# Hybrid encoder block: keys of memory heads 2 and 3 moved behind the query tiles, a12 loaded in another buffer, the last adds of the down-projection spread

## The chip, the cores and the metric

One core of a Trainium2 chip runs the whole kernel in one launch. The metric is device time in microseconds, lower is better; the kernel before takes 2694.26 us (median of three runs, 2693.18 to 2695.48).

## The reference, cut to what matters

The block works on 2048 tokens of width 1024, with a memory of 256 rows, in fp32:

```python
h  = rms_norm(x, mix_norm);  z = h @ w_in           # conv gates, q, k, v, g, low-rank gates
x += concat(convs, gated linear attention) @ w_out
hq = rms_norm(x, xa_norm) @ w_xq
km, vm = split(rms_norm(mem, mem_norm) @ w_xkv)     # 4 heads of 256
x += softmax(hq km' / 16) vm @ w_xo                 # memory cross-attention
x += square(relu(rms_norm(x, mlp_norm) @ w_up)) @ w_down
return rms_norm(x, final_norm)
```

## The kernel before, in words

Every fp32 operand of a product is split into a high part (a cast on ACT, L117) and a rest (a subtraction on DVE, L118); a product is then three matmuls per 128 rows (L145 to L147, `mm3`), so PE does three passes and is fed by one ACT and one DVE instruction per operand tile. Tokens come in four blocks of 512, in two halves (`hf`). A block is loaded in four tiles (`prep_load`), squared on ACT (L184) and folded on DVE (L188, L189), its norm is spread to all partitions by PE (`rstd_col` L161, `to_rows` L169, with a power on POOL, L153, in between), and `block_steps` scales it (eight L206 on DVE) and splits it (four casts on ACT, four L118 on DVE).

The prologue makes `zA`, the memory keys folded into the query weight. `kv_mm` (48 matmuls) makes a head's keys K0 to K3, `kv_out` (L552 and a split) scales them, `xa_key` multiplies them with two weights of `wxqT` in eight steps of six matmuls, and L565 evacuates each step. All four heads are made before `qk(0)`, which computes four query and key tiles for token blocks 0 and 1. Then come `lr_g` and `vg` (gates and values), `conv`, the V phase (`kv_mm` of `wxv` and `xa_value` for four heads, beside the preparation of blocks 2 and 3), `qk(1)`, the gated linear attention, and the cross-attention.

The MLP uses Strassen-like forms with seven products. `token_side` (up-projection) makes the token operands of a half; `quarter` loads a quarter of `x2d` and scales it; a12 is the last of the four quarters and takes its buffer `S2` (ring ST) after a11 has been used. In the down-projection `half_steps` yields 56 steps of up to 48 matmuls (L1243); `add` (L928) evacuates them into `acc`, sixteen tiles loaded from `x2d` by `load_acc`. POOL and DVE combine raw operands there. What is common to several quarters is collected in `sums` and added to `acc` by 24 adds on DVE after the steps. The last four feature rows of the hidden layer (REST) go through `column`: eight tiles of 12 matmuls for each of the token blocks, then `finish` scales and stores.

The order of work: PE's order is written out in the prologue, in the V phase and in the final columns (`manual_schedule`); the other engines, and PE elsewhere, are ordered by the scheduler, which fixes each engine's queue before the run. Every engine, and SP that issues the loads and stores, takes its queue in order: an instruction that waits holds all behind it.

Of the kernel before, what the change touches and what calls it, by code (L numbers as in the profile page):

```python
# [30 lines left out]
def block_kernel(ctx, tc, x, mem, wm, wv, wlg, wlog, wout, wxk, wxv, wxqT, wxo, wup, wdn,  # L31
# [195 lines left out]
    def qk(hf, blks, ws):  # L227
        t0 = hf * 1024
        for pr in range(2):
            for z, idx, sc in ((zk, 2 + pr, 1.0), (zq, pr, 0.125)):  # L230
                def ev(bi, ps, z=z, sc=sc):
                    t = T2()
                    nc.scalar.mul(t, ps, sc)
                    nc.sync.dma_start(z[pr][:, t0 + bi * TB:t0 + (bi + 1) * TB], t)
                mtiles([(idx, ev)], blks, ws)
                ws = None

# [511 lines left out]

    def block_sq(b, eng):  # L750
        xs = prep_load(x, b, lambda i: A2())
        return xs, fold(xs, A2, eng)

# [11 lines left out]
    with tc.manual_schedule(engines={EngineType.PE}):  # L765
        mts = [mem_part(0)]
        ws = [load_w(wxk[0])]
        mts.append(mem_part(1))
        ws.append(load_w(wxk[1]))
        nc.sync.dma_start(cst, consts)  # L770
        mps = kv_mm(wxk, 0, G4, ws)
        sq = fold([mt[:, 2 * j:2 * j + 2] for mt in mts for j in range(2)], lambda: T2(F32, (P, 2, NMEM)), nc.vector)
        nc.scalar.copy(rmem, to_rows(rstd_col(sq, PS), PS))
        K0 = kv_out(mps)
        K1 = kv_mm(wxk, 1, A4)
        xa_key(0, K0, G4)
# [4 lines left out]
        ws = [load_w(wxk[6 + j], T=A4) for j in range(2)]  # L781
        rc0 = rstd_col(sq0, PG)
        xa_key(1, K1, G4)
        with behind("dma", "act"):
            xs1, sq1 = block_sq(1, nc.vector)
        r0 = block_rows(rc0, PG)
        K2 = kv_out(K2)
        K3 = kv_mm(wxk, 3, A4, ws)
        xa_key(2, K2, G4)
        blks = [block_steps(xs0, r0)]  # L790
        rc1 = rstd_col(sq1, PG)
        K3 = kv_out(K3)
        r1 = block_rows(rc1, PG)
        xa_key(3, K3, G4)
        w0 = [load_w(wm[2])]
        blks.append(block_steps(xs1, r1))
    qk(0, blks, w0)
    vg(0, blks, lr_g(0, blks))
    conv(0, blks, range(4))
    with tc.manual_schedule(engines={EngineType.PE}):  # L800
        V0 = kv_mm(wxv, 0, G4)
        V1 = kv_mm(wxv, 1, G4)
        V0 = kv_out(V0)
        xa_value(0, V0, G4)
        with behind("dma", "act"):
            xs0, sq0 = block_sq(2, nc.vector)
        V1 = kv_out(V1)
        V2 = kv_mm(wxv, 2, G4)
        rc0 = rstd_col(sq0, PG)
        xa_value(1, V1, G4)  # L810
        with behind("dma", "act"):
            xs1, sq1 = block_sq(3, nc.vector)
        r0 = block_rows(rc0, PG)
        V2 = kv_out(V2)
        V3 = kv_mm(wxv, 3, G4)
        xa_value(2, V2, G4)
# [397 lines left out]
    def load_acc(ds):  # L1214
        for d in ds:
            for c in range(2):
                acc[d][c] = A4()
                nc.sync.dma_start(acc[d][c], x2d[d * P:(d + 1) * P, c * 1024:(c + 1) * 1024])

    halves = [slice(0, TB), slice(TB, 2 * TB)]  # L1220
    steps = half_steps()
    ahead = [next(steps)]
    acc = [[None, None] for _ in range(KT)]
    load_acc(range(4))
    sums = [A4(F32, (P, 2, TB)) for _ in range(4)]
    for i in range(14 * len(GROUPS)):
        while len(ahead) < 3:
            ahead.append(next(steps, None))
        first, p, c, w, x = ahead.pop(0)
        if i == 0:  # L1230
            load_acc(range(4, KT))
        n = len(x)
# [4 lines left out]
        for d in range(4):  # L1237
            ds = slice(d * P, (d + 1) * P)
            ps = banks[d]
            for k in range(n):  # L1240
                wh, wl = w[k][0][:, ds], w[k][1][:, ds]
                for l, r in ((wh, x[k][0]), (wh, x[k][1]), (wl, x[k][0])):
                    nc.tensor.matmul(ps, l, r, start=not chained and k == 0 and l is wh and r is x[k][0],  # L1243
                                     stop=k == n - 1 and l is wl, skip_group_check=chained)
            o11, o21 = (acc[d][c][:, h] for h in halves)
            o12, o22 = (acc[d + 4][c][:, h] for h in halves)
# [4 lines left out]
            for o in {1: (u,), 2: (o11,), 6: (u,), 5: (o22,), 3: (o12,), 7: (o21, o22), 4: (o21,)}[p]:  # L1251
# [6 lines left out]
    def rest_u(b):  # L1258
        got = []
        for i in range(0, 4, 2):  # L1260
            t = (RAW() if i == 0 else CV()[:, :D]).rearrange("p (j t) -> p j t", j=2)
            for j in range(2):
                f = REST[i + j]
                nc.sync.dma_start(t[:, j], zu[f * P:(f + 1) * P, b * TB:(b + 1) * TB])
            hi, lo = (A4(F32R, (P, 2, TB)) for _ in range(2))
            split(t, hi, lo)
            got += [(hi[:, j], lo[:, j]) for j in range(2)]
        return got

    ur = [rest_u(0)]  # L1270
    wr = [load_w(wdn[f], T=G4) for f in REST]
# [17 lines left out]

    def column(us, c, cs, squares, between):  # L1290

        qs = []
        n = cs.stop - cs.start
        o = cs.start % TB
        for d in range(KT):
            ds = slice(d * P, (d + 1) * P)
            ps = (PG if d % 2 == 0 else PS)()[:, :n]
            for j in range(4):
                mm3(ps, (wr[j][0][:, ds], wr[j][1][:, ds]), (us[j][0][:, o:o + n], us[j][1][:, o:o + n]), j == 0, j == 3)
# [24 lines left out]
    with tc.manual_schedule(engines={EngineType.PE, EngineType.DVE}):  # L1324
        for n, (c, cs) in enumerate(blocks):
            if n + 1 < 4:
                ur.append(rest_u(n + 1))
            sq = column(ur[min(n, 3)], c, cs, nc.vector if n == len(blocks) - 1 else nc.gpsimd, todo)
            for _ in todo or ():
# [64 lines left out]
```

## Time and profile before

| | us |
|---|---|
| median of three runs | 2694.26 |
| profiled execution | 2702.45 |
| its span | 2700.7 |
| PE busy | 2592.5 (96%) |
| DVE busy | 1626.4 (60%) |
| ACT busy | 933.2 (35%) |
| POOL busy | 259.6 (10%) |

The profiled execution is 1.75 us longer than its span, and 8.2 us above the median of the runs. PE is the engine that is busy nearly all of the span, so the table is read by what is left of it: 108.2 us in which PE is idle, a good part of it in a few places that the rows below show, and the stretches in which PE runs at the lower of its two clock levels.

### The profile page before, as it was taken

Reading aid. Unit: us, or ns where it says so; the run is one execution under the profiler, and the core shown is the slowest. Engines: PE = TensorE matmul, PEld = TensorE weight load, DVE = VectorE, ACT = ScalarE, POOL = GpSimd, SP = SyncE. Lnnn points to the kernel's source line nnn. Section 1 sums busy time; section 2 is a strip of 40 time slices with the busy share of each in tenths; the row PEclk is TensorE's granted clock in tenths of the full one; section 3 lists DMA queues with packets and bytes.
Section 4 is the critical chain, followed back from the end, with each engine's and each line's share of the span. In section 5 each row is a group of like instructions: output and inputs, shape, how many; then the busy total and the mean of one; then the engine's idle time right before and its main releaser. Section 6 shows DMA issues by size and latency. Waiting matters only on the chain.

```text
span 2700.7 us, 34654 instructions
## 1 busy us (share of the span) xinstructions
PE 2592.5 (96%) x13560; PEld 2207.7 (82%) x13560; DVE 1626.4 (60%) x2502; ACT 933.2 (35%) x1432; POOL 259.6 (10%) x178
## 2 busy tenths in 40 slices
PE   7999999989989999999999999899999899999998
PEld 7898888877777787989997888788887788888877
DVE  6512363467766455344467657766556768687975
ACT  5411153434435343232234333433333223222232
POOL 0000000000010000000000000000003224243223
PEclk9999999999999999999999999999999999999999
DMA  7512354224435452111134333343338664555233
GB/s 253 179 61 69 101 185 162 81 88 121 135 104 175 145 183 94 52 43 48 48 115 166 106 113 106 110 159 107 112 121 290 220 197 150 179 168 174 95 106 110
DMA packets 198309, 353.26 MB, mean 131 GB/s; under 512 B 17345, under 2 KB 73793, under 8 KB 198145
## 3 DMA queue, kind: packets, MB, share of 16 engines
q1 hardware_dynamic: 198144, 351.05, 39.9%
q8 instruction: 106, 1.74, 0.3%
q14 instruction: 59, 0.48, 0.1%
HBM read 262.90 MB, written 88.08 MB: 130 GB/s over the span
## 4 chain that ended last, share of the span: by engine, by line
PE 77%; DVE 10%; DMA 6%; ACT 3%; issue 2%; POOL 0%; SPq 0%; DVEq 0%; POOLq 0%; ACTq 0%
PE ps L1013 12%; PE ps L145 9%; PE ps L147 9%; PE ps L146 9%; PE pg L1243 9%; PE ps L1243 9%; PE pg L1013 9%; PE pg L145 3%; PE pg L147 3%; PE pg L146 2%; DVE a L118 2%; DMA gt<-zv 2%; DVE g L118 1%; DVE st L474 1%; DVE g L400 1%
## 5 line engine op out<-in xcount | busy, mean ns | idle before, releaser
L145 PE MATMUL ps<-a,a 128*128 128x512 f32 (+1 forms) x840 | 306.0, 364 | 6.5 <-DVE t L249 5.9
L146 PE MATMUL ps<-a,a 128*128 128x512 f32 (+1 forms) x840 | 306.0, 364 | 0.0
L147 PE MATMUL ps<-a,a 128*128 128x512 f32 (+1 forms) x840 | 305.1, 363 | 0.0
L1243 PE MATMUL pg<-a,g 128*128 128x512 f32 x1176 | 288.6, 392 | 10.1 <-DVE a L928 7.2
L1013 PE MATMUL ps<-a,g 128*128 128x512 f32 x1152 | 284.5, 392 | 7.4 <-ACT a L117 4.4
L1243 PE MATMUL ps<-a,g 128*128 128x512 f32 x1176 | 284.8, 389 | 0.0
L1013 PE MATMUL pg<-a,g 128*128 128x512 f32 x1152 | 279.6, 390 | 1.7 <-ACT g L117 1.1
L1243 PEld LDWEIGHTS pg<-a,g 128*128 128x128 f32 x1176 | 221.7, 189 | 59.1 <-issue 7.6
L1013 PEld LDWEIGHTS ps<-a,g 128*128 128x128 f32 x1152 | 217.4, 189 | 54.1 <-ACT a L117 5.0
L1243 PEld LDWEIGHTS ps<-a,g 128*128 128x128 f32 x1176 | 220.8, 188 | 45.9
L1013 PEld LDWEIGHTS pg<-a,g 128*128 128x128 f32 x1152 | 216.4, 188 | 48.4 <-ACT g L117 2.0
L117 ACT CAST a<-raw 128x1024 fp32r<-128x1024 f32 (+1 forms) x126 | 127.9, 1022 | 346.0 <-PE ps L1243 112.1
L118 DVE TENSOR_TENSOR a<-raw,a 128x1024 fp32r<-128x1024 f32 (+1 forms) x126 | 156.0, 1246 | 117.3 <-ACT a L117 115.9
L117 ACT CAST g<-gt 128x512 fp32r<-128x512 f32 x180 | 103.8, 618 | 349.0 <-PE pg L1013 197.2
L145 PEld LDWEIGHTS ps<-a,a 128*128 128x128 f32 x840 | 161.6, 192 | 32.6 <-DVE t L249 4.7
L146 PEld LDWEIGHTS ps<-a,a 128*128 128x128 f32 x840 | 162.0, 193 | 23.2 <-issue 0.2
L147 PEld LDWEIGHTS ps<-a,a 128*128 128x128 f32 x840 | 161.7, 192 | 23.3 <-issue 0.2
L118 DVE TENSOR_TENSOR g<-gt,g 128x512 fp32r<-128x512 f32 x180 | 133.4, 780 | 44.7 <-ACT g L117 44.7
L928 POOL TENSOR_TENSOR gt<-gt,t 128x512 f32<-128x512 f32 x42 | 79.4, 1908 | 815.9 <-DMA t<-in_wdn 746.9
L928 DVE TENSOR_TENSOR t<-pg,t 128x512 f32<-128x512 f32 x64 | 44.2, 691 | 172.0 <-issue 126.3
L928 DVE TENSOR_TENSOR a<-pg,a 128x512 f32<-128x512 f32 (+1 forms) x128 | 84.1, 668 | 62.3 <-PE pg L1243 46.1
L118 DVE TENSOR_TENSOR g<-raw,g 128x1024 fp32r<-128x1024 f32 (+3 forms) x90 | 98.7, 1107 | 35.6 <-ACT g L117 35.5
(323 smaller groups left out, 5157.7 us busy)
## 6 DMA issues: line engine op xcount, KB each, us to landing
raw<-zu SPq DMA_DIRECT2D x64, 512.0 KB, 4.1
t<-in_wdn SPq DMA_DIRECT2D x84, 256.0 KB, 4.1
raw<-in_wm SPq DMA_DIRECT2D x32, 512.0 KB, 4.1
raw<-in_wup SPq DMA_DIRECT2D x32, 512.0 KB, 4.1
cv<-in_wup SPq DMA_DIRECT2D x32, 512.0 KB, 4.9
zu<-gt SPq DMA_DIRECT2D x64, 256.0 KB, 2.4
zu<-t SPq DMA_DIRECT2D x64, 256.0 KB, 3.9
cv<-zu SPq DMA_DIRECT2D x32, 512.0 KB, 5.0
```

The source lines that it names most:

```text
L117: mark["act"] = nc.scalar.copy(hi, src)
L118: nc.vector.tensor_tensor(out=lo, in0=src, in1=hi.bitcast(F32), op=ALU.subtract)
L145: nc.tensor.matmul(ps, lh, rh, start=first, stop=False)
L146: nc.tensor.matmul(ps, lh, rl, start=False, stop=False)
L147: mark["pe"] = nc.tensor.matmul(ps, ll, rh, start=False, stop=last)
L400: nc.vector.tensor_tensor_scan(out=Q[hf][:, sl], data0=reset, data1=K[hf][:, sl], initial=0.0, op0=ALU.mult, op1=ALU.add)
L474: nc.vector.scalar_tensor_tensor(out=St[r, a], in0=St[r, b], scalar=de[r, a:a + 1], in1=St[r, a], op0=ALU.mult, op1=ALU.add)
L928: eng.tensor_tensor(out=out, in0=a, in1=b, op=op)
L1013: nc.tensor.matmul(ps, W[w][:, ks], X[x][kt], start=first and kt + w + x == 0, stop=kt == 3 and w == 1, skip_group_check=not first)
L1243: nc.tensor.matmul(ps, l, r, start=not chained and k == 0 and l is wh and r is x[k][0], stop=k == n - 1 and l is wl, skip_group_check=chained)
```

## The change

Five edits. (1) In the prologue blocks 0 and 1 are loaded and folded earlier, only heads 0 and 1 have their keys made before `qk(0)`; heads 2 and 3 follow it. (2) `qk` takes all four weights at once and runs four tiles on block 0, then four on block 1, where before each tile ran on both blocks. (3) Block 2 is loaded, folded and normed around the last convolution group of the first half, and the V phase prepares only block 3. (4) In the second half's up-projection a12 is loaded with the other quarters into `R2` (rings RAW and CV). (5) In the down-projection the first and second half of `acc` are loaded at steps 0 and 2 (before: ahead of the loop and at step 0), the first REST operands are loaded two steps before the end, the 24 adds move into `column`, one a tile, and the first column is made in two passes over all eight PSUM banks.

```diff
@@ qk
-        for pr in range(2):
-            for z, idx, sc in ((zk, 2 + pr, 1.0), (zq, pr, 0.125)):
-                mtiles([(idx, ev)], blks, ws)
+        tiles = [(i, out(z, i % 2, sc)) for i, z, sc in ((2, zk, 1.0), (0, zq, 0.125), (3, zk, 1.0), (1, zq, 0.125))]
+        mtiles(tiles, blks, ws + [load_w(wm[i]) for i, _ in tiles[1:]])
@@ prologue
         K0 = kv_out(mps)
+        with behind("dma", "act"):
+            xs0, sq0 = block_sq(0, nc.vector)
         K1 = kv_mm(wxk, 1, A4)
         xa_key(0, K0, G4)
-        with behind("dma", "act"):
-            xs0, sq0 = block_sq(0, nc.vector)
-        K1 = kv_out(K1)
-        K2 = kv_mm(wxk, 2, A4)
...
+        K1 = kv_out(K1)
         r0 = block_rows(rc0, PG)
...
         blks = [block_steps(xs0, r0)]
+        xa_key(1, K1, G4)
+        w0 = [load_w(wm[2])]
         rc1 = rstd_col(sq1, PG)
...
     qk(0, blks, w0)
+    for h in (2, 3):
+        xa_key(h, kv_out(kv_mm(wxk, h, A4)), G4)
     vg(0, blks, lr_g(0, blks))
-    conv(0, blks, range(4))
+    conv(0, blks, range(3))
+    xs0, sq0 = block_sq(2, nc.vector, lambda dt=F32: G4(dt, (P, 2, TB)))
+    r0 = block_rows(rstd_col(sq0, PG), PG)
+    conv(0, blks, [3])
+    blks = [block_steps(xs0, r0)]
@@ token_side
+        if hf == 1:
+            a12 = quarter(hf, 0, 1, R2())
         yield None
...
-        a12 = quarter(hf, 0, 1, S2())
+        if hf == 0:
+            a12 = quarter(hf, 0, 1, S2())
@@ down-projection
-    load_acc(range(4))
...
-        if i == 0:
-            load_acc(range(4, KT))
+        if i in (0, 2):
+            load_acc(range(2 * i, 2 * i + 4))
+        if i == 14 * len(GROUPS) - 2:
+            ur = [rest_u(0)]
+            wr = [load_w(wdn[REST[0]], T=G4)]
...
-    for d in range(4):
-        for c in range(2):
-            u = sums[d][:, c]
-            for o in (acc[d][c][:, halves[1]], acc[d + 4][c][:, halves[0]], acc[d + 4][c][:, halves[1]]):
-                add(o, o, u, eng=nc.vector)
@@ column
+        for d in range(KT if passes == 2 else 0):
+            pss.append((PG if d % 2 == 0 else PS)()[:, :n])
+            part(d, (0, 1))
         for d in range(KT):
...
+            part(d, (2, 3) if passes == 2 else range(4))
...
+            if (c, cs.start) != (1, TB) and n == TB:
+                if cs.start == TB or d >= 4:
+                    add(a, a, sums[d % 4][:, c])
+                elif d < 4:
+                    dd = d + 4 * c
+                    late = acc[dd][1][:, halves[1]]
+                    add(late, late, sums[d][:, 1])
             add(a, ps, a)
```

On ACT the prologue's queue changes. In the kernel before, the first instructions from the norm of the memory rows (`rows`) on stand behind all the weights of heads 0 and 1: a4_231 and a4_261 are the weights of K1, g4_291 and g4_297 those of head 0's keys.

```order
L117 CAST a4_231<-raw_229 128x1024
L117 CAST a4_261<-raw_259 128x1024
L117 CAST g4_291<-raw_289 128x1024
L117 CAST g4_297<-raw_295 128x1024
L773 COPY rows_82<-ps_218 128x256
L117 CAST t2_222<-t2_224 128x512
L184 ACTIVATE a4_393<-a4_381 128x1024
L184 ACTIVATE a4_395<-a4_384 128x1024
L184 ACTIVATE a4_398<-a4_387 128x1024
L184 ACTIVATE a4_401<-a4_390 128x1024
```

In the changed kernel K1's weights are called a4_255 and a4_285, head 0's g4_315 and g4_321, and block 0 is a4_228 to a4_237.

```order
L776 COPY rows_82<-ps_218 128x256
L117 CAST t2_222<-t2_224 128x512
L184 ACTIVATE a4_240<-a4_228 128x1024
L184 ACTIVATE a4_242<-a4_231 128x1024
L184 ACTIVATE a4_245<-a4_234 128x1024
L184 ACTIVATE a4_248<-a4_237 128x1024
L117 CAST a4_255<-raw_253 128x1024
L117 CAST g4_315<-raw_313 128x1024
L117 CAST a4_285<-raw_283 128x1024
L117 CAST g4_321<-raw_319 128x1024
```

The copy of the row norm, the split of K0 and the four squares of block 0 moved ahead of the casts of K1's weights.

On DVE, head 1's second weight is called g4_483 (high) and g4_484 (rest); in the kernel before the same weight is g4_502, and nothing of a block's scaling stands ahead of it.

```order
L552 TENSOR_TENSOR t2_407<-ps_228,rows_82 128x512
L118 TENSOR_TENSOR a4_481<-raw_478,a4_480 128x1024
L118 TENSOR_TENSOR t2_406<-t2_407,t2_405 128x512
L151 TENSOR_SCALAR sm_489<-pg_484 128x4
L118 TENSOR_TENSOR g4_496<-raw_493,g4_495 128x1024
L118 TENSOR_TENSOR g4_502<-raw_499,g4_501 128x1024
```

In the changed kernel t2_439 is the rest of K1, and a4_228 to a4_237 are block 0.

```order
L118 TENSOR_TENSOR t2_439<-t2_440,t2_438 128x512
L206 SCALAR_TENSOR_TENSOR a4_228<-a4_228,vec_76,t2_444 128x512 x2
L206 SCALAR_TENSOR_TENSOR a4_231<-a4_231,vec_76,t2_444 128x512 x2
L118 TENSOR_TENSOR a4_452<-a4_228,a4_451 128x1024
L206 SCALAR_TENSOR_TENSOR a4_234<-a4_234,vec_76,t2_444 128x512
L118 TENSOR_TENSOR a4_458<-a4_231,a4_457 128x1024
L206 SCALAR_TENSOR_TENSOR a4_234<-a4_234,vec_76,t2_444 128x512
L206 SCALAR_TENSOR_TENSOR a4_237<-a4_237,vec_76,t2_444 128x512 x2
L118 TENSOR_TENSOR a4_464<-a4_234,a4_463 128x1024
L118 TENSOR_TENSOR g4_484<-raw_481,g4_483 128x1024
L118 TENSOR_TENSOR a4_470<-a4_237,a4_469 128x1024
```

The rest of head 1's second weight moved behind all eight scalings and three of the four splits of block 0.

In the V phase of the kernel before, value head 3 starts from t2_3407, and t2_3408 is made from its result in PSUM; a4_3071 to a4_3080 are block 2, the first of the two blocks that this phase prepares, and a4_3223 to a4_3232 block 3.

```order
L118 TENSOR_TENSOR a4_3380<-a4_3074,a4_3379 128x1024
L118 TENSOR_TENSOR a4_3386<-a4_3077,a4_3385 128x1024
L206 SCALAR_TENSOR_TENSOR a4_3080<-a4_3080,vec_76,t2_3247 128x512
L151 TENSOR_SCALAR sm_3402<-pg_3397 128x4
L552 TENSOR_TENSOR t2_3408<-ps_3260,rows_82 128x512
L118 TENSOR_TENSOR g4_3422<-raw_3419,g4_3421 128x1024
L118 TENSOR_TENSOR a4_3392<-a4_3080,a4_3391 128x1024
L118 TENSOR_TENSOR t2_3407<-t2_3408,t2_3406 128x512
L118 TENSOR_TENSOR g4_3428<-raw_3425,g4_3427 128x1024
L118 TENSOR_TENSOR a4_3474<-raw_3471,a4_3473 128x1024
L206 SCALAR_TENSOR_TENSOR a4_3223<-a4_3223,vec_76,t2_3412 128x512 x2
```

In the V phase of the changed kernel value head 3 starts from t2_3438, block 3 is a4_3083 to a4_3092, and wm's raw_3443 and raw_3502 are the first weights of `qk(1)`; this is DVE's queue ahead of t2_3438.

```order
L206 SCALAR_TENSOR_TENSOR a4_3089<-a4_3089,vec_76,t2_3293 128x512
L118 TENSOR_TENSOR a4_3368<-a4_3086,a4_3367 128x1024
L206 SCALAR_TENSOR_TENSOR a4_3089<-a4_3089,vec_76,t2_3293 128x512
L206 SCALAR_TENSOR_TENSOR a4_3092<-a4_3092,vec_76,t2_3293 128x512 x2
L118 TENSOR_TENSOR g4_3452<-raw_3449,g4_3451 128x1024
L118 TENSOR_TENSOR a4_3374<-a4_3089,a4_3373 128x1024
L118 TENSOR_TENSOR g4_3458<-raw_3455,g4_3457 128x1024
L118 TENSOR_TENSOR a4_3380<-a4_3092,a4_3379 128x1024
L554 TENSOR_TENSOR t2_3439<-ps_3300,rows_82 128x512
L118 TENSOR_TENSOR a4_3446<-raw_3443,a4_3445 128x1024
L118 TENSOR_TENSOR a4_3505<-raw_3502,a4_3504 128x1024
L118 TENSOR_TENSOR t2_3438<-t2_3439,t2_3437 128x512
```

The rest of value head 3 moved behind all of block 3's scaling; in the kernel before it stands ahead of it.

## Rows read from the trace of the kernel before

**Rows 1.** The page, part 1: busy us, share of the span, instructions.
```profile
PE 2592.5 (96%) x13560; PEld 2207.7 (82%) x13560; DVE 1626.4 (60%) x2502; ACT 933.2 (35%) x1432; POOL 259.6 (10%) x178
```

**Rows 2.** Window of the prologue: us, busy PE, PEld, DVE, ACT, POOL, clock, DMA, GB/s.
```profile
22.16:82.42 60.26, 51.86 (x372) 49.38 (x370) 42.25 (x49) 40.48 (x63) 2.02 (x2) 0.89 0.73 239
```

**Rows 3.** PE timeline, prologue: start, us, instruction, count, idle before and releaser.
```profile
22.16 0.36 PE L145 MATMUL ps<-gt,a 128*128 128x256 f32 x1
...
27.90 0.28 PE L145 MATMUL ps<-t,g 128*128 128x256 f32 x1
...
34.70 0.39 PE L145 MATMUL ps<-gt,a 128*128 128x256 f32 x1
...
42.52 0.39 PE L145 MATMUL ps<-t,g 128*128 128x256 f32 x1 [1.30 <-ACT g L117]
...
82.42 0.40 PE L145 MATMUL ps<-a,a 128*128 128x512 f32 x1
...
125.97 0.29 PE L145 MATMUL ps<-g,a 128*128 128x288 f32 x1
```

**Rows 4.** ACT timeline, prologue, same columns.
```profile
22.97 0.36 ACT L773 COPY rows<-ps 128x256 f32<-128x256 f32 x1
24.96 0.62 ACT L117 CAST t<-t 128x512 fp32r<-128x512 f32 x1 [1.63 <-DVE t L552]
25.49 3.90 ACT L184 ACTIVATE a<-a 128x1024 f32<-128x1024 f32 x4
...
29.87 1.05 ACT L117 CAST a<-raw 128x1024 fp32r<-128x1024 f32 x1
```

**Rows 5.** DVE timeline, prologue, same columns.
```profile
27.53 3.89 DVE L188 TENSOR_TENSOR a<-a,a 128x1024 f32<-128x1024 f32 x3 [1.22 <-ACT a L184]
...
32.06 1.22 DVE L118 TENSOR_TENSOR a<-raw,a 128x1024 fp32r<-128x1024 f32 x1
...
76.35 3.39 DVE L206 SCALAR_TENSOR_TENSOR a<-a,vec,t 128x512 f32<-128x512 f32 x5
...
87.79 1.23 DVE L118 TENSOR_TENSOR a<-a,a 128x1024 fp32r<-128x1024 f32 x1 [1.11 <-ACT a L117]
```

**Rows 6.** PE timeline, V phase: its start, two waits, its end.
```profile
351.08 0.28 PE L145 MATMUL ps<-gt,g 128*128 128x256 f32 x1
...
383.74 0.58 PE L145 MATMUL ps<-gt,g 128*128 128x256 f32 x1 [2.81 <-ACT g L117]
...
400.56 0.82 PE L169 MATMUL pg<-cst,sm 128*128 128x128 f32 x5 [1.34 <-POOL sm L153]
...
452.27 0.29 PE L145 MATMUL ps<-g,a 128*128 128x288 f32 x1
```

**Rows 7.** PE timeline, up-projection of the second token half.
```profile
1744.73 0.51 PE L1013 MATMUL ps<-a,g 128*128 128x512 f32 x1 [4.41 <-ACT a L117]
1746.11 5.06 PE L1013 MATMUL ps<-a,g 128*128 128x512 f32 x11 [0.88 <-DVE a L118]
```

**Rows 8.** PE timeline, start of the down-projection.
```profile
2102.80 4.95 PE L1243 MATMUL pg<-a,g 128*128 128x512 f32 x12 [7.19 <-DVE a L928]
2107.58 2.92 PE L1243 MATMUL ps<-a,g 128*128 128x512 f32 x12
```

**Rows 9.** DVE by form, 2068 to 2093 us: count, busy us, mean ns, idle.
```profile
L118 DVE TENSOR_TENSOR g<-gt,g 128x512 fp32r<-128x512 f32 x4 | 8.5, 2174 | 1.0 <-ACT g L117 1.0
...
L928 DVE TENSOR_TENSOR a<-ps,a 128x512 f32<-128x512 f32 x2 | 1.4, 677 | 0.0
```

**Rows 10.** PE timeline, end of the down-projection.
```profile
2588.93 0.50 PE L146 MATMUL pg<-a,g 128*128 128x512 f32 x1 [1.87 <-DVE a L118]
2591.27 0.50 PE L147 MATMUL pg<-a,g 128*128 128x512 f32 x1 [1.83 <-DVE g L118]
...
2594.19 0.63 PE L145 MATMUL ps<-a,g 128*128 128x512 f32 x1
```

**Rows 11.** DVE timeline, end of the down-projection.
```profile
2593.46 8.51 DVE L928 TENSOR_TENSOR a<-a,a 128x512 f32<-128x512 f32 x14
```

More of the change, by code (lines that the diff above doesn't have):

```diff
@@ L748, in block_kernel, with block_sq @@
     XR = lambda i: RAW((P, 2, TB)) if i % 2 == 0 else CV()[:, :D].rearrange("p (j t) -> p j t", j=2)
[L750 to L752 removed]
+    def block_sq(b, eng, T=None):
+        T = T or A2
+        xs = prep_load(x, b, lambda i: T())
+        return xs, fold(xs, T, eng)
     def block_rows(rc, PT):
@@ L803, in block_kernel @@
         V0 = kv_out(V0)
+        with behind("dma", "act"):
+            xs1, sq1 = block_sq(3, nc.vector)
         xa_value(0, V0, G4)
-        with behind("dma", "act"):
-            xs0, sq0 = block_sq(2, nc.vector)
         V1 = kv_out(V1)
         V2 = kv_mm(wxv, 2, G4)
-        rc0 = rstd_col(sq0, PG)
         xa_value(1, V1, G4)
-        with behind("dma", "act"):
-            xs1, sq1 = block_sq(3, nc.vector)
-        r0 = block_rows(rc0, PG)
+        rc1 = rstd_col(sq1, PG)
         V2 = kv_out(V2)
+        r1 = block_rows(rc1, PG)
         V3 = kv_mm(wxv, 3, G4)
+        blks.append(block_steps(xs1, r1))
         xa_value(2, V2, G4)
-        blks = [block_steps(xs0, r0)]
-        rc1 = rstd_col(sq1, PG)
         V3 = kv_out(V3)
-        r1 = block_rows(rc1, PG)
+        w0 = [load_w(wm[2])]
         xa_value(3, V3, G4)
-        w0 = [load_w(wm[2])]
-        blks.append(block_steps(xs1, r1))
     qk(1, blks, w0)
@@ L1218, in load_acc, with rest_u @@
                 nc.sync.dma_start(acc[d][c], x2d[d * P:(d + 1) * P, c * 1024:(c + 1) * 1024])
+    def rest_u(b):
+        got = []
+        for i in range(0, 4, 2):
+            t = (RAW() if i == 0 else CV()[:, :D]).rearrange("p (j t) -> p j t", j=2)
+            for j in range(2):
+                f = REST[i + j]
+                nc.sync.dma_start(t[:, j], zu[f * P:(f + 1) * P, b * TB:(b + 1) * TB])
+            hi, lo = (A4(F32R, (P, 2, TB)) for _ in range(2))
+            split(t, hi, lo)
+            got += [(hi[:, j], lo[:, j]) for j in range(2)]
+        return got
     halves = [slice(0, TB), slice(TB, 2 * TB)]
@@ L1244, in block_kernel @@
                                      stop=k == n - 1 and l is wl, skip_group_check=chained)
-            o11, o21 = (acc[d][c][:, h] for h in halves)
-            o12, o22 = (acc[d + 4][c][:, h] for h in halves)
+            out_ = lambda dd, h: acc[dd][c][:, halves[h]]
             u = sums[d][:, c]
@@ L1250, in block_kernel @@
                 continue
-            for o in {1: (u,), 2: (o11,), 6: (u,), 5: (o22,), 3: (o12,), 7: (o21, o22), 4: (o21,)}[p]:
+            goes = {2: ((d, 0),), 5: ((d + 4, 1),), 3: ((d + 4, 0),), 7: ((d, 1), (d + 4, 1)), 4: ((d, 1),)}
+            for o in [u] if p in (1, 6) else [out_(*g) for g in goes[p]]:
                 if p == 4:
@@ L1255, in block_kernel @@
                     add(o, ps, o)
[L1258 to L1271, printed above, removed]
-    for d in range(4):
-        for c in range(2):
-            u = sums[d][:, c]
-            for o in (acc[d][c][:, halves[1]], acc[d + 4][c][:, halves[0]], acc[d + 4][c][:, halves[1]]):
-                add(o, o, u, eng=nc.vector)
+    wr += [load_w(wdn[f], T=G4) for f in REST[1:]]
     def final_sums(sq, n, PT):
@@ L1288, in final_scale, with column @@
         nc.sync.dma_start(out[d * P:(d + 1) * P, c * 1024 + cs.start:c * 1024 + cs.stop], a)
-    def column(us, c, cs, squares, between):
+    def column(us, c, cs, squares, between, passes=1):
         qs = []
@@ L1294, in column, with part @@
         o = cs.start % TB
+        pss = []
+        def part(d, js):
+            ds = slice(d * P, (d + 1) * P)
+            for j in js:
+                mm3(pss[d], (wr[j][0][:, ds], wr[j][1][:, ds]), (us[j][0][:, o:o + n], us[j][1][:, o:o + n]), j == 0, j == 3)
+        for d in range(KT if passes == 2 else 0):
+            pss.append((PG if d % 2 == 0 else PS)()[:, :n])
+            part(d, (0, 1))
         for d in range(KT):
[L1296 to L1299, printed above, removed]
+            if passes == 1:
+                pss.append((PG if d % 2 == 0 else PS)()[:, :n])
+            part(d, (2, 3) if passes == 2 else range(4))
+            ps = pss[d]
             a = acc[d][c][:, cs]
+            if (c, cs.start) != (1, TB) and n == TB:
[5 more added lines that the diff above has]
+                    add(late, late, sums[d][:, 1])
             add(a, ps, a)
@@ L1327, in block_kernel @@
                 ur.append(rest_u(n + 1))
-            sq = column(ur[min(n, 3)], c, cs, nc.vector if n == len(blocks) - 1 else nc.gpsimd, todo)
+            sq = column(ur[min(n, 3)], c, cs, nc.vector if n == len(blocks) - 1 else nc.gpsimd, todo,
+                        2 if n == 0 else 1)
             for _ in todo or ():
```

19 lines of the change are left out of this document (6 added, 13 removed).

## The prediction

> **What bounds the kernel now.** I read the page's busy times first: PE works 2592.5 of 2700.7 us [rows 1], so whatever moves the time must change one of two things on PE: its idle time, 108.2 us in all, or the stretches at its lower clock. Then the waits of PE by place, to see where that idle time lies. Five places matter here: the prologue, the V phase, one point of the up-projection, and both ends of the down-projection. For each I ask what the wait ended on, and what stands in that engine's queue ahead of it after the change.
>
> The prologue from K1's first matmul to the end of `qk(0)` runs from 22.16 to 125.97, 103.8 us [rows 3]. Its last part, eight query tiles, takes 125.97 - 82.42 = 43.55, that is 5.44 a tile without a wait. The part before has 60.26 us, 51.86 of them busy: 8.40 idle, at a mean granted clock of 0.89 [rows 2]. One head's keys take 27.90 - 22.16 = 5.74, and its `xa_key` 34.70 - 27.90 = 6.80, of which 48 matmuls are 5.7 and the rest waits [rows 3]. Three heads' keys (17.2), four `xa_key` (22.8) and about 2.4 of norms are 42.4 at the full clock, so 51.86 - 42.4 = 9.5 us of the busy time is the lower clock. I keep this balance: 42.4 + 43.55 of work, 8.4 idle, 9.5 slow clock.
>
> **Part by part. Prologue.** The work is the same after the change, so only idle and slow clock have to be found, by walking along PE's order and asking when each operand is ready.
>
> K1's first weight is cast on ACT behind the copy of the row norm, K0's split and four squares of block 0. Of these only the copy and split are needed by something near. The copy ran at 22.97, the split at 24.96, the squares from 25.49 for 3.90 [rows 4]. Without the casts ahead of them and without DVE's weight rests, I put copy and split about 1 us earlier: squares end near 28, the cast (1.05, [rows 4]) near 29. K1 starts at 29.0 instead of 22.16: 6.8 idle. Its rest stands on DVE behind the folds, three adds for 3.89 that follow the squares [rows 5], plus 1.22 for itself [rows 5]: 30.5, another 1.4 idle after two matmuls.
>
> After K1 and head 0's keys the norm of block 0 goes PE, DVE, POOL, PE: 1.3 us is such a wait elsewhere [rows 6], I take 2.0 with the scaling of K1 behind it. Then head 1's keys: their second weight's rest now follows, on DVE, all eight scalings (3.39 / 5 = 0.68 each, [rows 5]) and three splits (1.23, [rows 5]) of block 0, and takes 1.23 itself: 5.4 + 3.7 + 1.2 = 10.3. `xa_key` needs it at its sixth matmul, 0.7 us after its start, so 9.5 idle. In the kernel before a wait on such a weight here cost 1.30 [rows 3].
>
> The second query tile needs wm0, whose split is queued on ACT and DVE behind all of block 1's preparation, and that waits for block 1's norm, which PE makes after head 1's keys. Norm 2.0, preparation 12.7 (from 76.35 to 87.79 + 1.23 for the same eight scalings and four splits, [rows 5]), split 1.2: 15.9 after the keys' end. Of these, 2.0 is PE's own wait for the norm. In the other 13.9 PE has only tile 1 (5.44): 8.5 idle, of which I take 7.5, as two idle times on ACT lie in that 12.7; with the norm 9.5. Before, block 1 was needed only after the first tile on block 0, too, but head 3's keys stood in front as cover; with keys 2 and 3 behind the tiles that cover is gone.
>
> K2 and K3 now follow each other through `kv_out` with nothing in between: add, cast and subtraction on DVE, ACT, DVE are 0.69 + 0.62 + 0.69 = 2.0 each (cast 0.62, [rows 4]; the DVE steps taken like a scaling, [rows 5]), 4.0 for both.
>
> Idle: 6.8 + 1.4 + 2.0 + 9.5 + 2.0 + 7.5 + 4.0 = 33.2. Slow clock: three long stalls end in K1, in head 1's keys and in tile 2; before the slow stretches cost 9.5 together behind shorter stalls, and I take 9.5 again. `lr_g` then starts at 22.16 + 42.4 + 43.55 + 33.2 + 9.5 = 150.8 instead of 125.97: **+25**. Some of these waits overlap what I count as wait inside `xa_key`; I take **+24**. Bounds: with half the idle time and no more slow clock than half, 33.2 / 2 + 4.8 - 17.9 = +3.5; with a weight load that queues behind stores on SP (head 1's second weight does) another 5: +30.
>
> **V phase.** It lasts 452.27 - 351.08 = 101.2 us [rows 6]. It had waits of 2.81 and 1.34 [rows 6] and smaller ones; all its work at the full clock is sixteen 5.44-us pieces (eight query tiles, four values, four `kv_mm` of 5.74), 88, and the norms, so some 9 us are lost. Block 2 is then ready before, which takes its share away. But value head 3 now stands on DVE behind block 3's eight scalings, its splits and wm's weights: 8 x 0.68 + 8 x 1.23 + 0.7 = 16 from the norm of block 3, while PE has value head 3's product (5.74) and value 2 (5.44) as cover: 16 - 11.2 = 5, and 1.3 for the norm, with the slow clock behind. I take **0**, bounds -6 (no new wait) and +5 (its load, behind a store on SP, comes late as well).
>
> **Up-projection.** a12 was loaded into a buffer that a11 had to leave; PE waited 4.41 + 0.88, and 11 matmuls behind it took 5.06 [rows 7] against 2.92 for 12 at full speed [rows 8], 2.4 more. With its own buffer all of it goes: -7.7, **-8** with a small wait on a weight after it. Low bound -9; if a12's early load pushes the next weights, whose buffers RAW and CV it takes, the saving shrinks to -4.
>
> **Start of the down-projection.** PE waited 7.19 for a DVE evacuation and lost 2.0 in the next 12 matmuls (4.95 against 2.92, [rows 8]). DVE was late because its operations with both inputs in SBUF took 2.17 us for 128x512 [rows 9] while POOL combined tokens. POOL's combinations for the token side come earlier in its queue after the change, and half of `acc` is loaded later. I take most of the 9.2 back, less about 2 for the first weights, which on SP now stand behind a load of `acc` whose buffer is freed only by the last up-projection products: **-4**, from -9 (all goes) to +2 (the backlog stays and only the queue is longer).
>
> Here the same rows bear on the 24 adds too. Beside POOL, evacuations that read PSUM kept 677 ns, splits from SBUF took three times as long [rows 9]. The Trainium skill, GPSIMD Engine Reference, section Specifications, says that POOL shares its SBUF interface with VectorE and that instructions with two SBUF inputs contend; by it the stretch returns in the columns. The trace agrees on which instructions it meets. The 24 adds have two SBUF inputs, and in the columns they run beside POOL's folds, where before they ran in one piece.
>
> **End of the down-projection.** The last products end, and the REST weights were split late: 1.87 and 1.83 and some 0.8 more, then a tile at the lower clock from 2594.19, 12 matmuls in 4.8 instead of 2.8 [rows 10]: 6.5 us lost. DVE, which those splits waited for, was busy with sums and evacuations; 14 of the 24 adds took 8.51 [rows 11], 0.61 each. After the change the first operands are split before, and pass one of the first column needs only two weights. **-5**; from -7 to +2. The 24 adds cost 0.61 x 24 = 14.6 us of DVE, hidden beside PE tiles of 2.8 us with some 1.4 of DVE work each; stretched to 2 us each, by the factor of [rows 9], they would stand 0.6 over in a tile, 14 us over 24 tiles. POOL is busy for 10% of the span [rows 1], so I take 0 and leave the 14 to the third rival.
>
> **Sum.** +24 + 0 - 8 - 4 - 5 = +7. On the profiled execution, 2702.45, that is 2709; the profiled one stands 8.2 above the median of the runs, and on the median it is 2694.3 + 7 = **2701**.
>
> **Rivals.** First, the forecast: the prologue loses some 24, more than the four gains give back, 2701.
> Second, on the other side: the waits in the prologue are no longer than before. It is one mechanism: each of the three long waits rests on one instruction that the queue holds behind a block's work; if loads, squares and norms of the blocks land early enough, that work is done while K1 and head 0 still run, and the weights are late by 1 or 2 us each, as before [rows 3]. Then the prologue is at most +6 (its `kv_out` waits, 4.0, and 2), the sum 6 - 17 = -11: 2683. For it speaks that DMA moved 239 GB/s in that window and ACT was busy for 40 of 60 us [rows 2], so there is room; against it, that the norm of block 1 is made behind head 1's keys on PE, so its work can't be early. It decides when `lr_g` starts before 144.
> Third: the prologue loses as forecast, and the gains at the ends of the down-projection turn into nothing, since DVE's evacuations stay behind splits, or behind adds that POOL's folds stretch: +24 + 0 - 8 = +16, 2710. For it speaks that the chained products need DVE at the same points as before; against it that a backlog of 7.19 came from one crowd of POOL work [rows 8, 9].
>
> **How the numbers follow.** A measurement here can tell 0.2%, 5.4 us, from no change. Forecast 0.60, second 0.22, third 0.18. The forecast's own range is 2692 to 2709; of its 0.60, 0.37 are above 2699.7, 0.20 within 5.4 of before, 0.03 below 2688.9. The second gives 0.18 faster and 0.04 same, the third is slower. Faster 0.21, same 0.24, slower 0.55. Range 2683 to 2713: it takes in the second's point and the third's with 3 above it.
>
> **What would show it.** Right: in the profile after, an idle time of 6 to 9 us ahead of K1's first matmul, ended by the cast of its weight on ACT; 8 to 10 us in head 1's keys, ended by a DVE rest of `wxqT`; 6 to 9 us ahead of the second query tile; `lr_g` between 144 and 155. The 4.4 and 7.2 us waits gone, and L1243 without a gap over 1 us near its end. Wrong: `lr_g` before 135, or a V phase over 106 us, or a wait of more than 5 us in the first two products of the down-projection.

## The result, and the profile after

The changed kernel takes 2707.19 us (median of five runs, 2704.82 to 2709.70) against 2693.41 for the kernel before (five runs). The ratio is 1.0049, 95% interval 1.0034 to 1.0064: slower by 13.8 us or 0.5%. The profiled execution has a span of 2703.0 us, 2.3 above that of the first profile of before. That pair understates the change: a second profile of the unchanged kernel (first experiment below) has a span of 2693.7, and some 6 of the 7 us between the two profiles of before lie between the second `lr_g` and the up-projection. I therefore compare stages with the second profile of before.

| stage, from PE's timeline | before, 1st | before, 2nd | after | after - 2nd |
|---|---|---|---|---|
| start to V phase | 351.1 | 351.1 | 375.9 | +24.9 |
| V phase | 101.2 | 101.4 | 104.2 | +2.9 |
| to the up-projection | 956.6 | 950.7 | 954.1 | +3.5 |
| up-projection, to the first down product | 625.7 | 625.3 | 617.9 | -7.4 |
| steps of the down-projection | 550.3 | 550.1 | 539.3 | -10.9 |
| columns and stores | 115.8 | 115.2 | 111.5 | -3.7 |
| span | 2700.7 | 2693.7 | 2703.0 | +9.3 |

The 9.3 us of two executions and the 13.8 of ten runs are not the same number; the executions of one kernel differ by 5 us among themselves, and the +3.5 in the middle is within what two profiles of before differ by. In that stage it is not the waits that differ. These are the two profiles of before, first and second, over it (us, busy us of PE, PEld, DVE, ACT, POOL, then clock, DMA share, GB/s):

```profile
452.27:1408.90 956.63, 910.19 (x5478) 791.56 (x5476) 528.89 (x1039) 346.13 (x574) 33.61 (x46) 0.98 0.31 99
```

```profile
452.41:1403.06 950.65, 903.77 (x5477) 786.55 (x5476) 528.88 (x1039) 346.24 (x574) 33.55 (x46) 0.98 0.31 100
```

PE is idle for 46.4 and 46.9 us, but the same matmuls keep it busy for 6.4 us more in the first. That is its clock: from 800 to 900 and from 1000 to 1100 the granted clock is 0.98 in the first and 1.00 in the second. The changed kernel has 44.5 us idle and 909.6 busy there, so its +3.5 is slower clock too, and no wait.

The prologue, PE's timeline of the changed kernel; columns are start, us, instruction, count, and in brackets the idle time ahead with what ended it.

```profile
28.41 0.58 PE L145 MATMUL ps<-gt,a 128*128 128x256 f32 x1 [6.57 <-ACT a L117]
...
30.63 0.58 PE L147 MATMUL ps<-gt,a 128*128 128x256 f32 x1 [1.43 <-DVE a L118]
...
49.05 0.58 PE L146 MATMUL ps<-t,g 128*128 128x256 f32 x1 [1.70 <-DVE t L118]
...
58.89 0.58 PE L147 MATMUL ps<-t,g 128*128 128x256 f32 x1 [7.66 <-DVE g L118]
...
79.26 0.80 PE L145 MATMUL ps<-a,a 128*128 128x512 f32 x1 [5.39 <-ACT a L117]
...
126.27 0.50 PE L145 MATMUL ps<-t,g 128*128 128x256 f32 x2 [1.48 <-ACT t L117]
...
139.57 0.62 PE L145 MATMUL ps<-t,g 128*128 128x256 f32 x3 [1.58 <-ACT t L117]
...
428.19 0.80 PE L145 MATMUL ps<-g,t 128*128 128x512 f32 x1 [8.09 <-ACT t L117]
```

Where K1 started at 22.16 without a wait [rows 3], it now waits 6.57 for its cast on ACT and 1.43 for its rest on DVE; head 1's keys wait 7.66 for a weight's rest, the second query tile 5.39 for the cast of its weight `wm[0]` (wm0 from here on), and each of the two moved heads some 1.5 for `kv_out`. The last row is in the V phase. The same window as in [rows 2] shows the price in one row (us, busy us of PE, PEld, DVE, ACT, POOL, then clock, DMA share, GB/s).

```profile
22.16:82.42 60.26, 35.13 (x207) 31.16 (x208) 42.14 (x48) 35.52 (x48) 2.02 (x2) 0.77 0.43 137
```

PE did 207 matmuls where it did 372 [rows 2], at a granted clock of 0.77 against 0.89. DVE's busy time is as before: its work was not more, it only stood in another order.

Of the waits that were to go, those at a12 [rows 7] and at the start of the down-projection [rows 8] are gone. This is the list of PE's waits from the first down product to the last (us in total, times, the longest).

```profile
PE pg L1257 <- ACT a L117: 0.8, 1, 0.8
PE pg L1257 <- DVE g L118: 0.2, 1, 0.2
```

Nothing over 1 us is left there. The columns begin without a wait too, against [rows 10], but DVE has more to do in them, as its timeline in the changed kernel shows:

```profile
2632.23 1.40 DVE L1283 SCALAR_TENSOR_TENSOR a<-a,vec,pg 128x512 f32<-128x512 f32 x2
2633.55 1.48 DVE L925 TENSOR_TENSOR a<-a,a 128x512 f32<-128x512 f32 x1
2635.12 0.69 DVE L925 TENSOR_TENSOR a<-ps,a 128x512 f32<-128x512 f32 x1
2635.73 1.40 DVE L1283 SCALAR_TENSOR_TENSOR a<-a,vec,pg 128x512 f32<-128x512 f32 x2
2637.05 1.48 DVE L925 TENSOR_TENSOR a<-a,a 128x512 f32<-128x512 f32 x1
2638.63 0.69 DVE L925 TENSOR_TENSOR a<-pg,a 128x512 f32<-128x512 f32 x1
```

A tile's share of DVE is 0.69 for the evacuation, 1.40 for two scalings of the column before, and 1.48 for an add that took 0.61 (start to start) in a row without POOL [rows 11]. The period is 3.5 us, where PE needs 2.7 for a tile. PE has no wait for these evacuations, though: its waits in the columns are for folds and powers, 5.7 us in all, against 2.7 in the kernel before once its first column has its operands.

### The profile page after: what moved, and what is told of

It reads as the page before. It is cut to its first block, busy times and chain, and to the rows that moved or that the text cites. A ratio compares the mean times of both kernels' runs of the same rounds, so it can differ in the third digit from the quotient of the medians.

```text
span 2703.0 us, 34701 instructions
## 1 busy us (share of the span) xinstructions
PE 2586.8 (96%) x13560; PEld 2201.9 (81%) x13560; DVE 1629.6 (60%) x2502; ACT 934.3 (35%) x1432; POOL 259.2 (10%) x178
## 4 chain that ended last, share of the span: by engine, by line
PE 79%; DVE 10%; DMA 4%; ACT 3%; issue 2%; POOL 1%; SPq 0%; DVEq 0%; POOLq 0%; ACTq 0%
PE ps L1013 12%; PE pg L1257 10%; PE ps L1257 10%; PE ps L145 10%; PE ps L147 10%; PE ps L146 9%; PE pg L1013 8%; PE pg L145 2%; PE pg L147 2%; PE pg L146 2%; DVE a L118 1%; DMA gt<-zv 1%; DVE st L476 1%; ACT a L117 1%; DVE g L402 1%
## 5 line engine op out<-in xcount | busy, mean ns | idle before, releaser
L153 POOL TENSOR_TENSOR sm<-sm,nhalf 128x2 f32<-128x2 f32 (+1 forms) x26 | 25.2, 968 | 996.9 <-DVE sm L151 996.9
L117 ACT CAST g<-raw 128x1024 fp32r<-128x1024 f32 (+3 forms) x90 | 85.6, 960 | 100.1 <-PE ps L146 17.7
```

Source lines behind the costliest of these rows:

```text
L117: mark["act"] = nc.scalar.copy(hi, src)
L153: nc.gpsimd.tensor_tensor(out=r, in0=v, in1=nhalf[:, :n], op=ALU.pow)
```

## The experiments

Each was timed together with the kernel before, in up to five rounds; ratios are to those runs. Stage times come from one profile each.

**The kernel before, profiled again.** No edit.

> The kernel before, unchanged, profiled a second time. The first profile's span (2700.7) stood 8 us over the median of its runs (2693.4), while that of the changed kernel (2703.0) stood under its own (2707.2). Theory: one of the waits read from the first profile is not in every execution; the wait of 7.2 us at the start of the down-projection is the candidate, since it hangs on POOL and DVE meeting. Then this profile lacks it and has a span near 2692. Rival: the surplus is spread over the whole execution (slow clock, transfers), and all waits of the first profile return.

2695.52 in one run, span 2693.7. PE's longest waits from 1730 to 2580:

```profile
PE pg L1243 <- DVE a L928: 7.2, 1, 7.2
PE ps L1013 <- ACT a L117: 4.9, 1, 4.9
PE pg L1243 <- DVE a L118: 1.2, 2, 0.6
```

The theory fell: the wait of 7.2 is in both. The rival holds, in that the waits return; the surplus is not spread over the whole, though, but sits between 452 and 1409, as busy time at a lower clock (shown with the result). What lowered the clock is open.

**The prologue and the query tiles alone.**

```diff
+            xs0, sq0 = block_sq(0, nc.vector)     # and the rest of the prologue's hunk
         K1 = kv_mm(wxk, 1, A4)
...
     qk(0, blks, w0)
+    for h in (2, 3):
+        xa_key(h, kv_out(kv_mm(wxk, h, A4)), G4)
```

> The kernel before with the changed prologue and the changed order of the query tiles alone. Theory (queues of ACT and DVE in the prologue cost some 24 us): lr_g starts at 150 instead of 126, time 2693.4 + 24 = 2717, and V phase and GLA unchanged behind it. Rival (the prologue's delay is made up later, since weights and blocks of later stages are ready earlier): lr_g at 150 but a time of 2707 or less.

2727.63, ratio 1.0107 (1.0091 to 1.0122), that is +29 us. The waits of the changed kernel stand there again (12.0 for ACT casts, 7.5 for the weight's rest), `lr_g` starts at 149.9, as the theory has it, and the V phase at 377.1, 26.1 late. Nothing is made up later: the rival falls. Of the 5 us beyond the theory 2.5 are in the V phase (103.8 against 101.4), whose `qk(1)` has the new order of tiles, though its other instructions are as before. The kernel below that has the new order with the prologue as before shows the same there (103.3).

**Everything but the prologue and the query tiles.**

```diff
+    conv(0, blks, range(3))
+    xs0, sq0 = block_sq(2, nc.vector, ...)        # and the V phase, a12, down-projection; prologue and qk as before
```

> The changed kernel with the prologue and the query tiles as before: block 2 in the convolutions, a12 and both ends of the down-projection changed. Theory: all of the loss is in the prologue; lr_g at 126, time 2707.2 - 24 = 2683, ratio to before 0.996. Rival (third of the prediction: the gains at the ends of the down-projection turn into nothing): 2688 to 2694.

2680.62, ratio 0.9942 (0.9930 to 0.9955): -15.6 us. With the +29 of the other half that makes +13, the measured change. The two halves add up, and the loss is in the prologue and the query tiles, which were changed together. It is 5 us under the theory's 0.996 because that half costs 29 and not 24; its V phase, 102.8, still has the wait of 8.1.

This half holds a smaller loss of its own. From `lr_g` to the V phase it takes 227.9 us, where the kernel before takes 225.1: the norm of block 2 that left the V phase costs PE 2.8 in the convolutions, and the V phase got 1.4 longer and not shorter. Without block 2's move (the kernel with a12 and down-projection alone, below) the ratio is 0.9926; the 4 us agree with the profiles, but the intervals overlap.

**The down-projection alone.**

```diff
+        if i in (0, 2):
+            load_acc(range(2 * i, 2 * i + 4))
+        if i == 14 * len(GROUPS) - 2:             # and the adds in column, first column in two passes
```

> The kernel before with the changed down-projection alone (loads of acc at steps 0 and 2, first rest operands early, adds in the columns, first column in two passes). By the two profiles the steps take 11 us less, the columns 3 less: 2680 if the first profile of before was typical. If its wait of 7.2 us is not in the usual execution: 2689 to 2691. Rival (adds stretched beside POOL hold the columns): 2693 or more.

2681.52, ratio 0.9947 (0.9934 to 0.9959): -14.3. Steps 539.2 us, columns 110.2 (550.1 and 115.2 before). That is what the waits of 7.2 and of the columns say, and more than the forecast's 4 + 5.

**K1 ahead of block 0.** The changed kernel, two statements swapped.

```diff
-        with behind("dma", "act"):
-            xs0, sq0 = block_sq(0, nc.vector)
         K1 = kv_mm(wxk, 1, A4)
+        with behind("dma", "act"):
+            xs0, sq0 = block_sq(0, nc.vector)
```

> The changed kernel with two statements of the prologue swapped: K1's product (and so its weights) ahead of the loads and squares of block 0. PE's order stays. On ACT K1's casts stand ahead of the squares again, and head 1's second weight comes ahead of block 0's scaling on DVE. Theory (the queue order on ACT and DVE is the cause, not that keys 2 and 3 left): the waits of 6.6 + 1.4 before K1 and of 7.7 in head 1's keys go, 15 us less, 2692. Rival (with two heads' keys fewer as cover, the blocks' preparation is late anyway, and the same time is waited ahead of the first or second query tile): 2703 or more.

2692.68, ratio 0.9983 (0.9974 to 0.9992), against 1.0049 for the changed kernel: 18 us less by the ratios. PE's longest waits from 20 to 140 in this kernel:

```profile
PE pg L169 <- POOL sm L153: 4.5, 2, 3.2
PE ps L145 <- ACT a L117: 3.6, 1, 3.6
PE ps L145 <- ACT t L117: 3.3, 2, 1.8
PE ps L145 <- ACT t L567: 2.9, 2, 1.6
```

The waits of 6.6 + 1.4 and of 7.7 are gone; two thirds of the second query tile's (3.6 of 5.4) and a longer one for block 1's norm (3.2) stay. Its V phase starts at 364.3, 11.6 earlier than the changed kernel's and 13.3 later than before; `lr_g` starts at 135.9, 10.0 later than before. So the theory holds for those two waits, which rest on queue positions and not on the missing cover. What is left fits the rival's mechanism, norms and splits of blocks 0 and 1 that are late with keys 2 and 3 behind the tiles, but no run separates it.

**Head 1's keys ahead of block 0's scaling.** The changed kernel, two statements swapped.

```diff
-        blks = [block_steps(xs0, r0)]
         xa_key(1, K1, G4)
+        blks = [block_steps(xs0, r0)]
```

> The changed kernel with the keys of head 1 written ahead of block 0's scaling. Head 1's second weight then stands on DVE behind two of the eight scalings and no split. K1's wait stays. Theory: the wait of 7.7 in head 1's keys falls to under 2, the time by 5 to 8, to 2700. Rival (the wait only moves to block 0's first query tile, which needs the scaling that is now later): 2706.

2701.44, ratio 1.0017 (1.0008 to 1.0026), 8.6 less than the changed kernel by the ratios. The wait of 7.7 is gone, a 1.6 us wait for the cast of the same weight is in its place, and the second tile's wait fell from 5.4 to 3.9, since block 1's norm is earlier too. K1's 6.6 stands. The span moved by only 1.2, a reminder that one profile pair is not the measure.

**a12 and the down-projection, prologue and V phase as before.**

```diff
+        if hf == 1:
+            a12 = quarter(hf, 0, 1, R2())         # with the down-projection's hunks
```

> The kernel before with two parts of the change: a12 in its own buffer, and the down-projection as changed. Theory: down-projection -16 as measured alone, a12 -7 as the profiles show, together -22 to -23, ratio 0.9915. Rival (a12's early load costs other loads what it gains): -16, as the down-projection alone.

2675.97, ratio 0.9926 (0.9914 to 0.9939): -20. a12 adds some 6 to the down-projection's 14.3; its stage is 618.2 in place of 625.3. The theory's -22 to -23 lies inside the interval, the rival's -16 just outside.

**Squares of the columns folded on DVE.** The kernel of the last experiment, with

```diff
-            sq = column(..., nc.vector if n == len(blocks) - 1 else nc.gpsimd, todo)
+            sq = column(..., nc.vector, todo)
```

> The same two parts, and the squares of the last columns are folded on DVE throughout, so POOL only makes the powers there. Theory (the 24 adds are stretched to 1.5 us because POOL folds beside them): the adds take 0.68 again and PE's waits for POOL in the columns (1.5, 0.5, 1.0) go, 1 to 3 us less than with POOL. Rival (the adds are slow for another reason): they stay at 1.5, and with the folds on DVE the columns get 3 or more longer.

2677.69, ratio 0.9930 (0.9917 to 0.9942), no different from with POOL. The 24 adds (DVE by form: busy us, mean ns), first in the changed kernel (1024 in the kernel of the last experiment),

```profile
L925 DVE TENSOR_TENSOR a<-a,a 128x512 f32<-128x512 f32 x24 | 24.6, 1023 | 0.0
```

then with the folds on DVE:

```profile
L928 DVE TENSOR_TENSOR a<-a,a 128x512 f32<-128x512 f32 x24 | 16.4, 683 | 0.0
```

The adds are stretched by POOL beside them: in the changed kernel itself the 11 adds that run beside no fold, or for 6% of their time at most, take 675 to 683 ns, and the other 13 take 956 to 1766. The time does not follow. The folds take 17.2 us more of DVE, where adds and splits give back 10.0, and PE's waits in the columns come to 6.1 us against 5.8: the first norm's power now makes it wait 2.7, in place of shorter waits.

**Value head 3 ahead of block 3's scaling.** All of the change but the prologue, and in the V phase

```diff
-        blks.append(block_steps(xs1, r1))
         xa_value(2, V2, G4)
...
         xa_value(3, V3, G4)
+        blks.append(block_steps(xs1, r1))
```

> The prologue as before, all other parts of the change (block 2 in the convolutions, query tiles four per block, a12, down-projection), and in the V phase the scaling of block 3 written behind value head 3, so that the cast of value 3's operand stands on ACT ahead of the second wm weight, whose load ended the 8.1 us wait of the changed kernel. Theory (that wait is one queue position): the V phase falls from 104.3 to 95 to 98, and the time to 3 to 5 us under the kernel with a12 and down-projection alone (0.9926 of before), 0.991. Rival (the wait moves to the first query tiles, which need block 3 or the weights): V phase 101 or more, 0.9926 or worse.

2677.52, ratio 0.9925 (0.9913 to 0.9938). The V phase is 97.5 us, as theory, and the wait of 8.1 is 2.1. The time is not better than 0.9926, because the stages ahead are longer than in the kernel with a12 and down-projection alone: `lr_g` starts at 127.2 and not at 124.5, and from there to the V phase block 2's norm costs its 2.7 again (227.8 us). With the old order of query tiles (next experiment) `lr_g` and V phase start 1.5 earlier; PE waits 1.6 here for wm0, and not there.

**The same with the old order of query tiles.** Each tile on both blocks again.

> The same with the query tiles in the old order, each tile on both blocks, so that block 3 is needed after one tile (5.4 us) and not after four (21.8). Theory: block 3, scaled behind value 3, is late by some 4 to 8 us, V phase 101 to 104. Rival (block 3 is ready in time either way, the order of the tiles does nothing): as the kernel with four tiles per block, within 1 us.

2674.18, ratio 0.9912 (0.9898 to 0.9927): the fastest here, 3.5 to 3.8 us under the two nearest kernels by the ratios, though the intervals overlap. The V phase took 96.4. Against the kernel with a12 and down-projection alone only 1.1 of it is ahead of the second `lr_g` (449.9 and 451.0), so that the move of block 2 gains these 4 us is not shown. My theory, that block 3 would be late after one tile, was wrong: from 353 to 450 PE waits for

```profile
PE ps L145 <- ACT t L117: 2.7, 1, 2.7
PE pg L169 <- POOL sm L153: 1.3, 1, 1.3
PE ps L147 <- DVE t L118: 0.3, 1, 0.3
```

and for nothing of block 3.

**The new order of query tiles with a12 and the down-projection.** Prologue and V phase as before.

> The kernel before with a12, the down-projection and the four tiles per block, prologue and V phase as before. Theory (the order of the tiles costs nothing and gives nothing where all four keys stand in front): 0.9926 of before, lr_g at 124 to 127. Rival (four weights loaded at once hold up the blocks' transfers): lr_g at 129 or later, 0.994 or more.

2680.51, ratio 0.9930 (0.9917 to 0.9944); `lr_g` at 129.0 against 124.5 with the old order. It points to a small loss, as the rival has it, not clear of noise in time. Of the 4.6 the profile puts 1.6 down to a wait ahead of the second tile for wm0's cast, which the old order does not have.

**Only the loads of acc moved.** The kernel before with

```diff
-    load_acc(range(4))
-        if i == 0:
-            load_acc(range(4, KT))
+        if i in (0, 2):
+            load_acc(range(2 * i, 2 * i + 4))
```

> The kernel before with only the loads of acc moved: its first half at step 0, its second at step 2. On POOL the first sums of tokens then stand ahead of the first combinations of weights, as in the changed kernel. Theory (the forecast's -4 for the start of the down-projection was too small, since this one move takes the whole wait of 7.2, the slow tile behind it and the small waits ahead): the steps last 539 to 541 us instead of 550, the end of the down-projection stays as before (115), the time is 9 to 11 less, ratio 0.9963. Rival (the 10.9 us come in part from the early rest operands and the adds that left the end of the steps): 4 to 6 less, steps 545.

2685.36, ratio 0.9956 (0.9942 to 0.9969): -11.9. The steps take 539.9 us, all of the 10 to 11 that the changed kernel gains there; the columns stay (114.7). DVE's timeline, before (second profile):

```profile
2067.79 7.41 DVE L118 TENSOR_TENSOR g<-gt,g 128x512 fp32r<-128x512 f32 x3
2075.11 4.57 DVE L118 TENSOR_TENSOR a<-st,a 128x1024 fp32r<-128x1024 f32 x2
2079.61 0.68 DVE L928 TENSOR_TENSOR a<-pg,a 128x512 f32<-128x512 f32 x1
```

and with this edit:

```profile
2064.75 1.37 DVE L118 TENSOR_TENSOR g<-gt,g 128x512 fp32r<-128x512 f32 x2 [7.72 <-ACT g L117]
2066.30 2.07 DVE L928 TENSOR_TENSOR st<-st,raw 128x1024 f32<-128x1024 f32 x1 [0.17 <-DMA raw<-zu]
2068.30 2.40 DVE L118 TENSOR_TENSOR g<-gt,g 128x512 fp32r<-128x512 f32 x2
2070.61 2.33 DVE L928 TENSOR_TENSOR st<-st,cv 128x1024 f32<-128x1024 f32 x1
2072.86 0.68 DVE L928 TENSOR_TENSOR a<-pg,a 128x512 f32<-128x512 f32 x1
```

The window from 2066 to 2086 in both kernels (columns as in the window above), before and then with this edit:

```profile
2066.00:2086.00 20.00, 18.85 (x82) 14.79 (x81) 20.00 (x11) 5.08 (x7) 20.00 (x9) 1.00 0.48 169
```

```profile
2066.00:2086.00 20.00, 20.00 (x90) 16.57 (x89) 19.72 (x16) 5.48 (x9) 13.77 (x6) 1.00 0.86 301
```

POOL was busy for all of that window and is now for 13.77 of 20. Its first sums of tokens are done at 2029 (at 2073 before), so DVE's operations that read two SBUF tiles meet it less: 16 instructions instead of 11 in the same 20 us. The evacuation that stood behind 12 us of splits is 7 us earlier, and PE has no wait there. The order on SP changed with it: the second load that those first sums need is issued at 2046.43 before, behind loads of `acc`, and at 2017.75 with this edit. So the edit is shown to be the cause; that it acts by POOL's order, and not by the earlier load, is argued.

## Why the prediction was right, by its steps

The sign and the mechanism were right: forecast 2701, measured 2707.2, inside the range. The forecast's change of +7 was half of the measured 13.8. That the stages of the profile sum to +9.3, so near to +7, is in part luck: the 7 us that the steps of the down-projection gained beyond the forecast stand against losses in the V phase, in the middle and behind `lr_g` that it did not have.

- Prologue, +24: +20.3, from the start of `lr_g`, which was at 125.97 before [rows 3] and is here in the changed kernel:

```profile
146.27 0.30 PE L145 MATMUL ps<-g,a 128*128 128x288 f32 x1
```

The windows from 22.16 to `lr_g`, before and then changed (columns as in [rows 2]), show that all of it is idle time of PE, 8.4 and 28.8 us at the same busy time:

```profile
22.16:125.97 103.81, 95.41 (x564) 85.44 (x563) 61.70 (x69) 59.07 (x87) 2.02 (x2) 0.93 0.69 223
```

```profile
22.16:146.27 124.11, 95.32 (x560) 84.22 (x561) 60.87 (x67) 59.26 (x83) 2.02 (x2) 0.89 0.48 151
```

The forecast had 33.2 idle and the same loss by the slow clock as before; by the busy time that loss is the same. Of its parts, K1's 6.8 + 1.4 are 6.57 + 1.43, head 1's weight 9.5 is 7.66 after 1.70 + 0.6 for other operands, tile 2's 7.5 is 5.39, the two `kv_out` 4.0 are 3.7, the two norms 4.0 are 2.1. The 24.9 in the first row of the table look like a hit, but 4.6 of them lie behind the start of `lr_g`: 1.2 is a wait for a weight in it, and 2.8 come with block 2's norm in the convolutions, as the kernel with the old prologue shows. The forecast took block 2 out of the V phase and booked it nowhere. Alone and in time the prologue with the query tiles cost 29.
- V phase, 0: +2.9. Half of its long wait was left out. The forecast put value 3 behind DVE's work on block 3 and took 5 us; the wait was 8.1, from 420.10 to 428.19. DVE's part is there: its add for value 3 comes behind splits of block 3.

```profile
422.73 0.68 DVE L554 TENSOR_TENSOR t<-ps,rows 128x512 f32<-128x512 f32 x1
```

ACT's timeline of the changed kernel shows the last link:

```profile
421.74 1.06 ACT L117 CAST a<-raw 128x1024 fp32r<-128x1024 f32 x1
426.57 1.04 ACT L117 CAST a<-raw 128x1024 fp32r<-128x1024 f32 x1 [3.77 <-DMA raw<-in_wm]
427.52 0.61 ACT L117 CAST t<-t 128x512 fp32r<-128x512 f32 x1
```

The cast of value 3's operand (0.61) stood behind the cast of a weight of the next stage, which waited 3.77 for its load. Right behind the add, by these durations, it would have been done at 424.0: that makes some 4.0 us of the wait DVE's, near the forecast's 5, and some 4.1 the load's. The forecast had a load behind a store on SP only as its bound, +5.
- a12, -8: -7.4 in the profile, some -6 in time.
- Start of the down-projection, -4: -10.9. This is the mis-sized term. The forecast took back only part of the 9.2 and took off 2 for weights late behind a load of `acc`; no such wait is there (0.8 and 0.2 in all the steps), and the experiment on `acc`'s loads shows all of it to come with their move.
- End, -5: -3.7. The first waits went as forecast; part was given back by the third rival's mechanism, adds stretched beside POOL's folds. The estimate of 2 us for such an add was 1.77 at most and 1.02 on the mean, and PE lost 3.0 us more to waits in the columns, not 14. The adds took 1023 ns with POOL's folds beside them and 683 without, while evacuations from PSUM stayed at 0.69 us. That bears out the rule that the Trainium skill, GPSIMD Engine Reference, section Specifications, gives: instructions of VectorE with two SBUF inputs contend with POOL.
- The second rival fell: `lr_g` starts at 146.3, where 144 was to decide, and all three long waits are there. Two of them, head 1's 7.66 and tile 2's 5.39, are just under the ranges given (8 to 10, 6 to 9).

Open: what lowered the clock in the +3.5 between the V phase and the up-projection, and the 4.5 us between the profiles' change and the runs'.

## What to carry to other kernels

A statement moved up in the program can move its instructions up in every queue, and not only in the one that it is meant for: here the squares of block 0 were needed after head 0's keys and stood on ACT ahead of the weights of K1, and one swap of two statements gave 18 us back. Work that is moved does not vanish, either: block 2's norm left the V phase and cost 2.8 us of PE in the convolutions. Before a stage is taken away as cover, list what it hid; here 25 us of keys had hidden two norms and two splits. And a gain measured for a whole change can be a sum of +29 and -16: the parts that won alone (`acc`'s loads moved, ratio 0.9956; a12 and down-projection, 0.9926; these with block 2 in the convolutions and value 3 ahead of block 3's scaling, 0.9912, which is not clear of the 0.9926) are worth more than the change.

## What the runs showed that I had not expected

- Moving two groups of loads back by up to two steps, with no work removed, took 11.9 us: the orders on SP and POOL changed, and with them how much DVE got done beside POOL.
- Taking POOL's folds away shortened the adds by a third (1023 to 683 ns) and made no difference that the timing can tell (ratios 0.9926 and 0.9930).
- Two executions of the same kernel differed by 6 us in one stage at equal waits (956.6 and 950.7 us), all of it in the clock that PE was granted.
